# A form preference for TensorE in a list scheduler, and a shorter layer-norm step, in a hybrid decoder kernel

## The chip, the core and the metric

The kernel runs on one core of one Trainium2 chip. The metric is the device time of one execution in microseconds (us), a median over runs. Engines are named as in the profile: PE (TensorE, matrix products), PEld (its weight loads), DVE (VectorE), ACT (ScalarE), POOL (GpSimd), SP (SyncE, which here only issues DMAs).

## The reference, cut to what matters

Two layers over a sequence of 1024 tokens of width 1024, batch 1, all float32. Layer 0 mixes tokens by a gated delta rule (8 heads of 128, causal convolution of 4 taps, chunked recurrence), layer 1 by a complex diagonal state space (S5, 64 groups of 16 channels). Beside either mixer runs a cross-attention of 4 heads into 256 memory tokens. Each layer ends like this:

```python
h = jnp.concatenate([mix, cross], axis=-1) @ w_o[i]
x = layer_norm(DN_ALPHA * x + h, ln1_g[i], ln1_b[i])
f = jnp.square(jax.nn.relu(x @ mlp_w1[i])) @ mlp_w2[i]
x = layer_norm(DN_ALPHA * x + f, ln2_g[i], ln2_b[i])
```

with

```python
mu = jnp.mean(xf, axis=-1, keepdims=True)
var = jnp.mean(jnp.square(xf - mu), axis=-1, keepdims=True)
return (xf - mu) * lax.rsqrt(var + 1e-5) * g + b
```

## The kernel before, in words

**Products.** Large products are split: each float32 operand becomes a high part in float32r (a copy on ACT) and a low part (a subtraction on DVE), and `mm3` (lines 394 to 399) issues three f32r products, high by high, high by low, low by high, into one PSUM bank. PE's large products therefore stand at lines 397, 398 and 399, mostly 128x128 by 128x512. Small products of the recurrences and all transposes stay in float32 ("f32" below): the delta rule's keys, queries and values (lines 1138 to 1343), its block inverse (line 1284), its recurrence (`gdn_recur`, lines 1429, 1432, 1435, 1441, 1447), the S5 products (lines 1875, 1945, 1970, 1971) and the transposes (lines 530, 1471, 1569 and others). An f32 product appears as two rows in the trace, a transpose as one. The profile prints both f32 and f32r as f32; the line tells them apart.

**Stages.** From 0 to about 670 us runs layer 0's mixer: projections of head h+1 are woven between the steps of head h's recurrence (`weave`). A step of the recurrence is a product whose result passes through DVE (R, line 1431, and S, line 1446) or ACT (e, line 1437) before the next. To about 780 us runs the output projection, to about 820 us the first layer norm (`block_end`), where transposes feed the first products of the MLP. The MLP of layer 0 lasts to about 1440 us, with S5 tables beside it; then follow S5, its gate and the attention of layer 1, the output projection, and from about 1910 us the MLP of layer 1. Its last part, `mlp_last`, makes 16 groups of 12 products, two for each of 8 tiles (tau 0 to 7) of 128 tokens. When the second group of a tile is done, `done` in `mlp_block` (line 2340) calls `layer_norm` and sends the tile out.

**Layer norm** (line 493). Two ways give the statistics. On DVE: two `bn_stats` (L509), `bn_aggr` (L510) for mean and variance, and a step that makes 1024 (variance + 1e-5) (L511). On ACT (where `junk` is given): sums (L502) and sums of squares (L505), with small steps on DVE (L503, L506). POOL then raises this number to -1/2 (L512). DVE makes two passes over the tile, (y - mean) g (L522) and times the power, plus b (L523). The gain g has been scaled by 32 on ACT, which makes good the 1024. For the very last tile the passes are L514 and L517 (in two halves), and the DMAs out are L518. In layer 1 tiles 5 and 6 take the ACT way.

**What sets the order.** The program is first written down, and then `settle` (line 62) reorders all instructions but the first few, on all engines at once, and fixes the order on each engine. It is a list scheduler with a cost model (`price`). PE's products get a due time, which is the sum of the costs of the products ahead of them in the written program; everything else must be done by the due times of what depends on it. At each step the scheduler picks for each engine among the instructions whose inputs are known (at most 40 us of due time ahead for PE):

```python
r = max(ready[x], s, free[e], due[x] - ahead if e != E.PE else 0.0)
...
other = 1.28 if sets[x] not in (None, table) else 0.0
k = (0, due[x] + other, r, x) if r <= free[e] + 0.1 else (1, r + other, due[x], x)
```

The smallest k wins: among those that can start within 0.1 us of the engine's being free, the one due first; if there is none, the one that can start first. `other` is the price of a change of ACT's function table. (For PE there is one charge already: 0.15 us on an f32 product that would leave a single f32r product between two f32 ones.) After a pick the successors become ready:

```python
same = e == E.PE and ins[y].engine == e
ready[y] = max(ready[y], r + (0.0 if x not in deps[y] else busy if same else length + lag + (margin if ins[y].engine == E.PE else 0.0)))
```

So a successor on the same engine other than PE is taken to be ready `length` + 0.05 us after its predecessor's start, where `length` is 0.08 us (DVE) or 0.1 us (ACT) more than the time for which the engine is busy.

Of the kernel before, what the change touches and what calls it, by code (L numbers as in the profile page):

```python
# [10 lines left out]
F32 = mybir.dt.float32  # L11
F32R = mybir.dt.float32r
AF = mybir.ActivationFunctionType
# [3 lines left out]
P = 128  # L17
# [16 lines left out]
class Trunk:  # L34
    def __init__(self, ctx, tc, a):
        self.tc = tc
        self.nc = nc = tc.nc
        self.a = a
        self.uid = 0
        self.turn = 0  # L40
        self.proj = 0
        self.soon = set()
        self.home, self.fixed = {}, set()
        self.cp = ctx.enter_context(tc.tile_pool(name="cp", bufs=1))
        self.sp = ctx.enter_context(tc.tile_pool(name="sp", bufs=1))
        self.ps = ctx.enter_context(tc.tile_pool(name="ps", bufs=1, space=bass.MemoryType.PSUM))
        self.dp = ctx.enter_context(tc.tile_pool(name="dp", bufs=1, space=bass.MemoryType.DRAM))
        self.ident = self.const("ident", [P, P])
        make_identity(nc, self.ident)
        self.const("pad", [P, 112])  # L50
        self.eps_ln = self.const("eps_ln", [P, 1])
        nc.gpsimd.memset(self.eps_ln, 1024 * 1e-5)
        self.mhalf = self.const("mhalf", [P, 4])
        nc.gpsimd.memset(self.mhalf, -0.5)
        self.half = self.const("half", [P, 4])
        nc.gpsimd.memset(self.half, 0.5)
# [5 lines left out]
    def settle(self, first, last, reach=0.0, ahead=15.0, passes=1, margin=0.0, late=0.0, hold=1e3):  # L62
# [118 lines left out]
        for _ in range(passes):  # L181
# [36 lines left out]
            while len(order) < n:  # L218
                first_ = None
                drift = free[E.PE] - due[turns[head]] if head < len(turns) else 0.0  # L220
                for e in names:
                    pick = None
                    for x in open_[e]:
                        if e == E.PE and x != turns[head] and due[x] > due[turns[head]] + reach - 1e-6:
                            continue
                        s = room(x) if fresh[x] else 0.0
                        if s is None:
                            continue
                        if e == E.SP:
                            s += 1  # L230
                        r = max(ready[x], s, free[e], due[x] - ahead if e != E.PE else 0.0)
                        if cost[x][2] > 1.5:
                            r = max(r, due[x] + drift - hold)
                        if e == E.PE and kind == "fr" and ins[x].ins[0].dtype == F32:
                            r += 0.15
                        other = 1.28 if sets[x] not in (None, table) else 0.0
                        k = (0, due[x] + other, r, x) if r <= free[e] + 0.1 else (1, r + other, due[x], x)
                        if pick is None or k < pick[0]:
                            pick = k, r, x
                    if pick and (first_ is None or pick[1:] < first_[1:]):  # L240
                        first_ = pick
                assert first_, f"no order: {len(order)} of {n}"
                r, x = first_[1:]
                e = ins[x].engine
                busy, length, moves = cost[x]
                if sets[x] not in (None, table):
                    table, busy, length = sets[x], busy + 1.28, length + 1.28
                if moves:
                    served = max(served, r + length - moves) + moves
                    length = served - r + late  # L250
                if port[x]:
                    r = max(r, locked)
                    locked = r + busy
                if e == E.PE:
                    lost += r - free[e]
                    kind = (kind + "fr"[ins[x].ins[0].dtype == F32R])[-2:]
                    gone.add(x)
                    while head < len(turns) and turns[head] in gone:
                        head += 1
                open_[e].remove(x)  # L260
                free[e] = r + busy
                order.append(x)
                for nm in fresh[x]:
                    t = self.home[nm][:2]
                    slots[t].remove(min(slots[t]))
                    turn[t].remove(nm)
                for y in after[x] + then[x]:
                    same = e == E.PE and ins[y].engine == e
                    ready[y] = max(ready[y], r + (0.0 if x not in deps[y] else busy if same else length + lag + (margin if ins[y].engine == E.PE else 0.0)))
                    wait[y] -= 1  # L270
                    if not wait[y]:
                        open_[ins[y].engine].append(y)
                for nm in uses(ins[x]):
                    if nm in users:
                        over[nm] = max(over[nm], r + length + (3 if ins[x].opcode == 'DMACopy' and e == E.Pool and self.home[nm][1] == 'gb' else 0.0))
                        todo[nm] -= 1
                        if not todo[nm] and nm not in behind and self.home[nm][:2] in slots:
                            slots[self.home[nm][:2]].append(over[nm] + lag)
# [214 lines left out]
    def layer_norm(self, y, gb, junk=None, last=None):  # L493

        nc = self.nc
        st = self.tile("st", [P, 2, 6], F32, "bn")
        halves = y if isinstance(y, list) else [y[:, c * HALF:(c + 1) * HALF] for c in range(2)]
        mv = self.tile("st", [P, 4], F32, "mv")
        if junk is not None:
            s = st.rearrange("p a b -> p (a b)")  # L500
            for c in range(2):
                nc.scalar.activation(junk, halves[c], AF.Copy, accum_out=s[:, c:c + 1])  # L502
            nc.vector.tensor_scalar(mv[:, 0:1], s[:, 0:1], s[:, 1:2], -1.0 / 1024, op0=ALU.add, op1=ALU.mult)  # L503
            for c in range(2):
                nc.scalar.activation(junk, halves[c], AF.Square, bias=mv[:, 0:1], accum_out=s[:, 4 + c:5 + c])  # L505
            nc.vector.scalar_tensor_tensor(mv[:, 2:3], s[:, 4:5], s[:, 5:6], self.eps_ln, op0=ALU.add, op1=ALU.add)  # L506
        else:
            for c in range(2):
                nc.vector.bn_stats(st[:, c, :], halves[c])  # L509
            nc.vector.bn_aggr(mv[:, 0:2], st)  # L510
            nc.vector.tensor_scalar(mv[:, 2:3], mv[:, 1:2], 1024.0, 1024 * 1e-5, op0=ALU.mult, op1=ALU.add)  # L511
        nc.gpsimd.tensor_tensor(mv[:, 3:4], mv[:, 2:3], self.mhalf[:, 0:1], op=ALU.pow)  # L512
        if last is not None:
            nc.vector.scalar_tensor_tensor(y, y, mv[:, 0:1], gb[0], op0=ALU.subtract, op1=ALU.mult)  # L514
            for c in range(2):
                c = slice(c * HALF, (c + 1) * HALF)
                nc.vector.scalar_tensor_tensor(y[:, c], y[:, c], mv[:, 3:4], gb[1][:, c], op0=ALU.mult, op1=ALU.add)  # L517
                nc.sync.dma_start(last[:, c], y[:, c])  # L518
            return
        parts = [(y, slice(0, 1024))] if not isinstance(y, list) else [(y[c], slice(c * HALF, (c + 1) * HALF)) for c in range(2)]  # L520
        for o, c in parts:
            nc.vector.scalar_tensor_tensor(o, o, mv[:, 0:1], gb[0][:, c], op0=ALU.subtract if junk is None else ALU.add, op1=ALU.mult)  # L522
            nc.vector.scalar_tensor_tensor(o, o, mv[:, 3:4], gb[1][:, c], op0=ALU.mult, op1=ALU.add)  # L523
# [1816 lines left out]
    def mlp_block(self, i, B, ahead, xd, side, out, more):  # L2340
        new = []

        def done(y, tau):
            if tau == 0:
                self.gb2 = self.load_gb(self.a["ln2_g"][i:i + 1], self.a["ln2_b"][i:i + 1])
                self.nc.scalar.activation(self.gb2[0], self.gb2[0], AF.Copy, scale=32.0)
                if more:
                    new.extend(self.new_xT())
            self.layer_norm(y[tau], self.gb2, self.psum("mm", "jk") if tau in ((), (5, 6))[i] else None, last=out[tau] if tau == 7 and not more else None)
            if tau < 7 or more:  # L2350
                self.nc.sync.dma_start(out[tau], y[tau])
            if more and tau == 7:
                self.last_x(y, new, more(new))
            elif more and tau < 6:
                self.transpose_x(y[tau], tau, new)
# [91 lines left out]
```

## Time and profile before

| | |
|---|---|
| median of 3 runs | 2513.36 us (2511.43 to 2513.53) |
| the profiled execution | 2512.02 us |
| its span, first to last instruction | 2510.3 us |
| mean granted TensorE clock | 0.998 |
| instructions | 36952 |

The profile is of one execution. Its page gives, for each engine, the time for which it was busy, and follows the chain of work that ended last back from the last instruction. Matrix products overlap in PE's pipeline: a product of 512 columns shows as 0.39 us, but the next one starts about 0.23 us later, so the distance from start to start is what counts. A wait is the idle time of an engine just before an instruction, put down to the instruction that released it last. A window row gives, for a stretch of time, each engine's busy time with the number of its instructions, and the granted clock.

### The profile page before, as it was taken

To read this page: it belongs to the slowest core of one execution; us is meant where nothing else is said; L and a number is where in the kernel's file an instruction comes from. 1 tells how busy PE (TensorE), PEld (TensorE's weight loads), DVE (VectorE), ACT (ScalarE), POOL (GpSimd) and SP (SyncE) were. 2 spreads that over 40 slices of the span, in tenths; PEclk is the share of its full clock that TensorE was granted. 3 is DMA by queue.
4 is the path that set the end of the run, shared out by engine and by line. 5 is a ranking of instruction groups with operands and counts; after the bars stand their busy time and mean duration, and the time that the engine had idled before them with its cause. 6 is when DMAs were issued, how large, how long until landed. Compare 5 with 4: busy or idle time off the path is not lost.

```text
span 2510.3 us, 36952 instructions
## 1 busy us (share of the span) xinstructions
PE 2471.1 (98%) x12181; PEld 2063.9 (82%) x12181; DVE 1969.6 (78%) x3676; ACT 1283.0 (51%) x2730; POOL 435.9 (17%) x673
## 2 busy tenths in 40 slices
PE   8999999999999999999999999999999999999998
PEld 6888887887887887888888888888887888888886
DVE  7786888777779798879988957786687666578788
ACT  6665555554556576554444244564365555544441
POOL 1232332414002023212210123112011000000000
PEclk9999999999999999999999999999999999999999
DMA  6464585767854567487454489669736434574532
GB/s 211 119 163 125 138 257 135 237 189 226 270 166 157 192 218 236 154 297 240 148 161 134 157 245 301 214 216 331 259 131 206 155 143 164 216 255 133 168 105 97
DMA packets 320769, 481.17 MB, mean 192 GB/s; under 512 B 110225, under 2 KB 141153, under 8 KB 320577
## 3 DMA queue, kind: packets, MB, share of 16 engines
q1 hardware_dynamic: 293056, 423.76, 51.9%
q0 software_dynamic: 25216, 50.86, 6.9%
q10 hardware_dynamic: 2304, 4.20, 0.4%
q8 instruction: 96, 1.57, 0.3%
q14 instruction: 97, 0.79, 0.1%
HBM read 321.91 MB, written 156.73 MB: 191 GB/s over the span
## 4 chain that ended last, share of the span: by engine, by line
PE 87%; DVE 5%; ACT 3%; DMA 2%; issue 2%; POOL 1%; SPq 0%; DVEq 0%; POOLq 0%; ACTq 0%
PE q L398 7%; PE q L397 7%; PE q L399 7%; PE tm L397 4%; PE tm L399 4%; PE tm L398 4%; PE pA L399 3%; PE pA L397 3%; PE pA L398 3%; PE wi L397 3%; PE wi L399 3%; PE wi L398 3%; PE pC L399 2%; PE pC L397 2%; PE pC L398 2%; PE pB L397 2%
## 5 line engine op out<-in xcount | busy, mean ns | idle before, releaser
L397 PE MATMUL q<-wkh,hkh 128*128 128x512 f32 x784 | 306.2, 391 | 0.7 <-ACT G L1886 0.7
L398 PE MATMUL q<-wkl,hkh 128*128 128x512 f32 x784 | 305.9, 390 | 0.5 <-DVE wkl L901 0.5
L399 PE MATMUL q<-wkh,hkl 128*128 128x512 f32 x784 | 305.4, 390 | 0.0
L900 ACT CAST wkh<-wr 128x512 fp32r<-128x512 f32 x168 | 104.9, 624 | 237.5 <-PE q L398 186.2
L512 POOL TENSOR_TENSOR mv<-mv,mhalf 128x1 f32<-128x1 f32 x32 | 26.7, 833 | 858.9 <-DVE mv L511 634.6
L397 PEld LDWEIGHTS q<-wkh,hkh 128*128 128x128 f32 x784 | 147.2, 188 | 32.2 <-ACT G L1886 1.6
L398 PEld LDWEIGHTS q<-wkl,hkh 128*128 128x128 f32 x784 | 147.3, 188 | 31.0 <-DVE wkl L901 1.1
L399 PEld LDWEIGHTS q<-wkh,hkl 128*128 128x128 f32 x784 | 147.2, 188 | 30.5
L901 DVE TENSOR_TENSOR wkl<-wr,wkh 128x512 fp32r<-128x512 f32 x168 | 115.5, 688 | 65.8 <-issue 55.6
L397 PE MATMUL wi<-xTh,wih 128*128 128x512 f32 x384 | 159.9, 416 | 0.2 <-ACT qT L1098 0.2
L398 PE MATMUL wi<-xTl,wih 128*128 128x512 f32 x384 | 152.6, 397 | 0.0
L399 PE MATMUL wi<-xTh,wil 128*128 128x512 f32 x384 | 152.4, 397 | 0.0
L901 DVE TENSOR_TENSOR hkl<-hr,hkh 128x512 fp32r<-128x512 f32 x196 | 133.9, 683 | 0.2 <-ACT hkh L900 0.2
L900 ACT CAST hkh<-hr 128x512 fp32r<-128x512 f32 x196 | 120.8, 616 | 1.3 <-DMA hr<-hd 1.2
L397 PE MATMUL tm<-so 128*128 128x512 f32 x280 | 109.8, 397 | 0.0
L1621 ACT CAST so<-or 128x1024 fp32r<-128x1024 f32 x70 | 72.0, 1049 | 59.5 <-DMA or<-wod 42.0
L1622 DVE TENSOR_TENSOR so<-or,so 128x1024 fp32r<-128x1024 f32 x70 | 84.5, 1220 | 16.1 <-ACT so L1621 16.0
L398 PE MATMUL tm<-so 128*128 128x512 f32 x224 | 88.2, 394 | 0.0
L399 PE MATMUL tm<-so 128*128 128x512 f32 x224 | 87.4, 391 | 0.0
L399 PEld LDWEIGHTS wi<-xTh,wil 128*128 128x128 f32 x384 | 72.7, 189 | 14.8
L397 PEld LDWEIGHTS wi<-xTh,wih 128*128 128x128 f32 x384 | 73.2, 191 | 12.5 <-ACT qT L1098 0.6
L398 PEld LDWEIGHTS wi<-xTl,wih 128*128 128x128 f32 x384 | 73.2, 191 | 11.6 <-issue 0.3
(588 smaller groups left out, 7381.8 us busy)
## 6 DMA issues: line engine op xcount, KB each, us to landing
hr<-hd SPq DMA_DIRECT2D x212, 256.0 KB, 2.8
wr<-in_w_dram SPq DMA_DIRECT2D x56, 512.0 KB, 5.0
hd<-u SPq DMA_DIRECT2D x92, 256.0 KB, 2.0
w1r<-in_w_dram SPq DMA_DIRECT2D x32, 512.0 KB, 3.5
hd<-hid SPq DMA_DIRECT2D x60, 256.0 KB, 2.3
hd<-p SPq DMA_DIRECT2D x60, 256.0 KB, 2.2
w1r<-in_w_dram SPq DMA_DIRECT2D x56, 256.0 KB, 3.6
wir<-in_w_in_dram SPq DMA_DIRECT2D x24, 512.0 KB, 3.9
```

The source lines that it names most:

```text
L397: mm(ps, a[0], b[0], start=start, stop=False, skip_group_check=onto)
L398: mm(ps, a[0], b[1], start=False, stop=False, skip_group_check=onto)
L399: mm(ps, a[1], b[0], start=False, stop=stop, skip_group_check=onto)
L512: nc.gpsimd.tensor_tensor(mv[:, 3:4], mv[:, 2:3], self.mhalf[:, 0:1], op=ALU.pow)
L900: nc.scalar.copy(hi, s)
L901: nc.vector.tensor_tensor(lo, s, f32(hi), op=ALU.subtract)
L1621: nc.scalar.copy(hi, r)
L1622: V.tensor_tensor(lo, r, f32(hi), op=ALU.subtract)
```

## The change

It has four parts.

1. In the scheduler, a product on PE whose form (f32 or f32r, by its first operand) differs from that of the product picked last is taken to be ready 0.035 us later, and `other` is 2.0 for it. Among the products that can start now it therefore goes behind one of the same form that is due up to 2.0 us later; where nothing can start now, behind one of the same form that can start up to 2.0 us (and the 0.035) later.
2. In the scheduler, a successor on the same engine (any engine, DMA issues excepted) counts as ready 0.06 us after its predecessor's busy time, if the predecessor stands in the last 60 us of the program.
3. In `layer_norm`, a [P, 2] constant (0, 1e-5) is added to (mean, variance) in one step, which writes the mean again and the variance plus 1e-5 side by side. The factor 1024 is gone in `mlp_block`, and with it the scaling of `gb2` by 32 on ACT. In `block_end` (y given as a list of halves) the sum of squares stays unscaled. Both passes read the mean from where the new step writes it; on the DVE way the first pass therefore comes behind this step.
4. In `mlp_block` of layer 1 tiles 3, 4 and 5 take the ACT way, instead of 5 and 6.

```diff
+        self.eps2 = self.const("eps2", [P, 2])
+        nc.gpsimd.memset(self.eps2[:, 0:1], 0.0)
+        nc.gpsimd.memset(self.eps2[:, 1:2], 1e-5)
...
                         other = 1.28 if sets[x] not in (None, table) else 0.0
+                        if e == E.PE and kind[-1:] != "fr"[ins[x].ins[0].dtype == F32R]:
+                            r, other = r + 0.035, 2.0
                         k = (0, due[x] + other, r, x) if r <= free[e] + 0.1 else (1, r + other, due[x], x)
...
-                    same = e == E.PE and ins[y].engine == e
-                    ready[y] = max(ready[y], r + (0.0 if x not in deps[y] else busy if same else length + lag + (margin if ins[y].engine == E.PE else 0.0)))
+                    same = ins[y].engine == e and (e == E.PE or not moves and spot[x] > now - 60.0)
+                    ready[y] = max(ready[y], r + (0.0 if x not in deps[y] else busy + (0.0 if e == E.PE else 0.06) if same else length + lag + (margin if ins[y].engine == E.PE else 0.0)))
...
-        mv = self.tile("st", [P, 4], F32, "mv")
+        mv = self.tile("st", [P, 6], F32, "mv")
...
-            nc.vector.scalar_tensor_tensor(mv[:, 2:3], s[:, 4:5], s[:, 5:6], self.eps_ln, op0=ALU.add, op1=ALU.add)
+            if isinstance(y, list):
+                nc.vector.scalar_tensor_tensor(mv[:, 1:2], s[:, 4:5], s[:, 5:6], self.eps_ln, op0=ALU.add, op1=ALU.add)
+            else:
+                nc.vector.tensor_scalar(mv[:, 4:5], s[:, 4:5], s[:, 5:6], 1.0 / 1024, op0=ALU.add, op1=ALU.mult)
+                nc.vector.tensor_tensor(mv[:, 1:2], mv[:, 4:5], self.eps2[:, 1:2], op=ALU.add)
...
-            nc.vector.bn_aggr(mv[:, 0:2], st)
-            nc.vector.tensor_scalar(mv[:, 2:3], mv[:, 1:2], 1024.0, 1024 * 1e-5, op0=ALU.mult, op1=ALU.add)
-        nc.gpsimd.tensor_tensor(mv[:, 3:4], mv[:, 2:3], self.mhalf[:, 0:1], op=ALU.pow)
+            nc.vector.bn_aggr(mv[:, 4:6], st)
+            nc.vector.tensor_tensor(mv[:, 0:2], mv[:, 4:6], self.eps2, op=ALU.add)
+        nc.gpsimd.tensor_tensor(mv[:, 3:4], mv[:, 1:2], self.mhalf[:, 0:1], op=ALU.pow)
...
-                self.nc.scalar.activation(self.gb2[0], self.gb2[0], AF.Copy, scale=32.0)
...
-            self.layer_norm(y[tau], self.gb2, self.psum("mm", "jk") if tau in ((), (5, 6))[i] else None, last=out[tau] if tau == 7 and not more else None)
+            self.layer_norm(y[tau], self.gb2, self.psum("mm", "jk") if tau in ((), (3, 4, 5))[i] else None, last=out[tau] if tau == 7 and not more else None)
```

## The prediction

> **What bounds the kernel.** I read the page first: how long, which engine, which chain.
>
> ```profile
> span 2510.3 us, 36952 instructions
> PE 2471.1 (98%) x12181; PEld 2063.9 (82%) x12181; DVE 1969.6 (78%) x3676; ACT 1283.0 (51%) x2730; POOL 435.9 (17%) x673
> PE 87%; DVE 5%; ACT 3%; DMA 2%; issue 2%; POOL 1%; SPq 0%; DVEq 0%; POOLq 0%; ACTq 0%
> ```
>
> PE is busy 98% of the span and holds 87% of the chain that ended last. A change of order removes no product, so it can win only what lies between the products. Second, the stages: a window without any f32 product, and the two windows in which the granted clock fell.
>
> ```profile
> 1910.00:2456.00 546.00, 545.77 (x2407) 451.35 (x2405) 382.74 (x609) 268.28 (x470) 0.00 (x0) 1.00 0.50 171
> 440.00:443.50 3.50, 3.50 (x15) 3.02 (x14) 2.82 (x7) 2.36 (x10) 3.50 (x7) 0.53 0.70 167
> 576.70:580.10 3.40, 2.79 (x11) 2.62 (x12) 3.31 (x6) 1.90 (x4) 3.02 (x5) 0.50 0.97 251
> ```
>
> Columns are the stretch, its length, then each engine's busy time with its count (PE first), and behind them the granted clock. An f32r product of 512 columns takes 546.00/2407 = 0.2268 us back to back, and that stage (MLP of layer 1) leaves nothing to win. The other two rows are half clock: 3.4 us each, so 1.7 us lost each.
>
> Third, the waits of PE, longest first; columns are total, times, longest.
>
> ```profile
> PE ba L1011 <- ACT xTh L993: 7.9, 2, 7.2
> PE po L1432 <- ACT on L1460: 4.3, 5, 2.4
> PE pe L1435 <- DVE R L1431: 3.0, 1, 3.0
> ...
> PE pe L1435 <- ACT e L1437: 0.6, 1, 0.6
> ```
>
> 7.2 us are the load of the input before the first product; the change does not touch that. The rest is mostly the recurrence of the gated delta rule (lines 1429 to 1447), f32 products in a chain through DVE and ACT, woven with f32r projections.
>
> **The change, part by part.** All durations are from the profiled execution: 2512.02 us, of which 2510.3 is the span. The median of the three runs, 2513.36, lies 1.34 above it; I take the sum off the median.
>
> *1. Fewer changes of form.* What does a change cost? One return (f32r, six f32 rows, f32r), and a long stretch of f32 alone:
>
> ```profile
> 432.02 0.61 PE L1319 MATMUL qt<-ident,qT 128*128 128x128 f32 x4
> 432.48 0.39 PE L1429 MATMUL ks<-S,kT 128*128 128x128 f32 x2
> 432.62 0.48 PE L399 MATMUL wi<-xTh,wil 128*128 128x512 f32 x1
> 432.93 0.40 PE L397 MATMUL wi<-xTh,wih 128*128 128x512 f32 x1
> ...
> 1479.07 0.38 PE L1970 MATMUL py<-s5t 128*128 128x128 f32 x2
> ...
> 1482.42 0.39 PE L1971 MATMUL py<-r,H 128*128 128x127 f32 x2
> ```
>
> From 1479.07 to 1482.42 stand 30 f32 rows, so 0.1117 us each. Six of them and one f32r product should take 6 x 0.1117 + 0.2268 = 0.897 us. From 432.02 to the second f32r product at 432.93 it took 0.91. The shown gap moves (the last f32 row seems to take 0.03, the next f32r product 0.31), but the whole return costs only about 0.013 us. The scheduler books 0.035 for each change, 0.07 for a return.
>
> PE's timeline has 342 such returns. The first and last groups of f32 are:
>
> ```profile
> 41.34 0.41 PE L1058 MATMUL gc<-early 128*128 128x64 f32 x2
> ...
> 1903.06 0.66 PE L530 MATMUL xt<-ident,y 128*128 128x128 f32 x4 [0.59 <-DVE xB L535]
> ```
>
> All of them together are worth 342 x 0.013 = 4.4 us, the end of what this part can give by itself. The rule lets a product wait while one of the other form is due within 2.0 us, so two f32 groups can merge if at most 2.0/0.2268 = 8 f32r products stand between them. 169 groups in the timeline are so placed: 2.2 us at most. Many are steps of one recurrence, where the second needs the first through ACT or DVE, and these cannot merge: 0 at least. I take half: **-1.1 us**.
>
> *2. Short waits on the recurrence.* With more slack a product can come into its place in time. The rows of two waits, one with f32r work at hand and one without:
>
> ```profile
> 264.21 0.46 PE L1435 MATMUL pe<-mix,iv 128*128 128x128 f32 x2 [0.57 <-ACT e L1437]
> ...
> 264.65 0.48 PE L399 MATMUL wi<-xTh,wil 128*128 128x512 f32 x1
> ...
> 502.44 0.49 PE L1432 MATMUL po<-S,gb 128*128 128x128 f32 x2 [0.88 <-ACT on L1460]
> ```
>
> At 264.21 the written order put a step of the chain ahead of projections that ran 0.44 us later: PE stood 0.57 us though there was work. Under the rule, in the midst of f32r products, the step goes behind them and its wait is covered. Of the waits above this holds for 0.6 (pe), and for po for 4.3 - 2.4 - 0.88 = 1.0: together 1.6 us. It is 0 if the f32r products are due more than 2.0 us later. I take two thirds: **-1.1 us**. What goes late instead is the chain itself; that is the second rival.
>
> *3. The end of the kernel: layer norm.* The last rows of DVE and of POOL; the first two columns are start and duration:
>
> ```profile
> 2499.94 1.28 DVE L522 SCALAR_TENSOR_TENSOR y<-y,mv,gb 128x1024 f32<-128x1024 f32 x1
> 2501.14 0.69 DVE L938 TENSOR_TENSOR y<-tm,y 128x512 f32<-128x512 f32 x1
> 2501.74 1.28 DVE L523 SCALAR_TENSOR_TENSOR y<-y,mv,gb 128x1024 f32<-128x1024 f32 x1
> 2502.93 0.69 DVE L509 BATCH_NORM_STATS2 bn<-y 128x6 f32<-128x512 f32 x1
> 2503.65 0.21 DVE L510 BATCH_NORM_AGGREGATE mv<-bn 128x2 f32<-128x12 f32 x1
> 2503.90 1.28 DVE L514 SCALAR_TENSOR_TENSOR y<-y,mv,gb 128x1024 f32<-128x1024 f32 x1
> 2505.10 0.15 DVE L511 TENSOR_SCALAR mv<-mv 128x1 f32<-128x1 f32 x1
> 2505.97 1.41 DVE L517 SCALAR_TENSOR_TENSOR y<-y,mv,gb 128x512 f32<-128x512 f32 x2 [0.73 <-POOL mv L512]
> ```
>
> ```profile
> 2500.17 1.46 POOL L512 TENSOR_TENSOR mv<-mv,mhalf 128x1 f32<-128x1 f32 x1 [5.08 <-DVE mv L506]
> 2505.39 0.55 POOL L512 TENSOR_TENSOR mv<-mv,mhalf 128x1 f32<-128x1 f32 x1 [3.76 <-DVE mv L511]
> ```
>
> The last add (2501.14) waits for no one but DVE; behind it stands the second pass of the tile before (2501.74, 1.19 us to the next start), then the statistics, the first pass L514, the eps step L511, the power on POOL, and L517, which starts 4.83 us after the add. The change does two things here. The bookkeeping for dependent steps on one engine in the last 60 us becomes 0.06 us, so the statistics count as ready right after the add and the second pass of the other tile no longer slips in between. And the eps step now comes ahead of L514, since it also writes the mean that L514 reads.
>
> New chain: add, statistics after 0.72 (as from 2502.93 to 2503.65), aggregate after 0.72, eps after 0.25 (as from 2503.65 to 2503.90), L514 after 0.25, together 1.94. The power beside a pass is slow: at 2500.17 it ended at 2501.63, 0.41 us after the pass that began at 2499.94 (end 2501.22). So L517 comes 1.28 + 0.41 = 1.69, with 0.03 to start 1.72, after L514, where it came 2.07 before. Sum 3.66 against 4.83: -1.2 if the displaced second pass finds a place ahead of the add, and with 1.20 us for it inside the chain 4.86, no gain. With the old order and only the eps step moved, 0.25 more and 0.35 less: -0.1. So 0 to -1.2; DVE is nearly full there, so I take the middle, **-0.6 us**.
>
> [...]
>
> The choice of tiles whose sums go to ACT (3, 4, 5 instead of 5, 6) takes one pair of statistics off DVE and gives tile 6 back to it; PE has no wait in the last 44 us, so only the tail sees it, inside the same 0 to -1.2.
>
> *4. The scaling of the layer-norm gain is gone.*
>
> ```profile
> L2346 ACT ACTIVATE gb<-gb x2: 1057/1058/1058, 1304.4 to 2429.8; 128x1024 f32<-128x1024 f32 x2
> ```
>
> Twice 1.06 us of ACT, 49% idle, and nobody waits for it (no wait on it in the views): 0. If that cover were gone, 2.1 us. The two further memsets of POOL lie ahead of the first load, under the 7.2 us: 0. The 0.035 in the scheduler is bookkeeping and issues nothing.
>
> **Sum**: -1.1 - 1.1 - 0.6 = -2.8, so 2513.4 - 2.8 = **2510.6**. Bounds of the terms: -(2.2 + 1.6 + 1.2) = -5.0 to 0. A new order also moves other waits under 1 us, on which I put +-2.5 as an estimate from the waits listed above: 2506 to 2515.
>
> **The rivals.**
>
> *The long stalls go too.* The waits of 2.4 and 3.0 us stand in the recurrence; if the new order happens to feed PE there, they and both half-clock windows go: 2.4 + 3.0 + 2 x 1.7 = 8.8, with the sum 2501.8. Against it: in the 3.0 us the wait is for DVE, and nothing in the rule speeds DVE.
>
> *Slower: the chain is held back.* The rule makes a step of the recurrence wait up to 2.0 us behind f32r products that are due later, even when it is the step on which everything else in that head hangs. When PE has nothing ready at all, the key adds the same 2.0 us, so it may idle for a product of its own form while one of the other form is ready sooner. While projections last, the delay is covered; where they run out, it becomes a stall. That happens now in six places (five waits of po, one of pe). Four held 2.0 us are 8.0; where a wait of about 0.9 grows past 2.4, the half clock follows, at two places 3.4. With parts 1 and 3: 8.0 + 3.4 - 1.7 = +9.7, 2523.1. It decides against the change from about three full holds and one loss of clock (7.7 us). For it: chain products wait longest now. Against it: a step overdue by more than 2.0 us still goes first.
>
> *Nothing moves.* Dependent f32 groups cannot merge and the order stays: only the tail, -0.1: 2513.3.
>
> *Longer runs of transposes cost clock.* A run of f32 transposes might count as rest, and each block end lose 1.7 us: +3.4 - 2.8, 2514.0. [...] The trace does not bear it out, within its lengths: at the end of the first block PE runs almost nothing but transposes for over 3 us (a timeline row, then the window, 20 PE rows), at a granted clock of 1.00.
>
> ```profile
> 802.88 1.25 PE L530 MATMUL xt<-ident,y 128*128 128x128 f32 x8 [0.26 <-DVE xB L535]
> ```
>
> ```profile
> 801.00:804.20 3.20, 2.68 (x20) 2.02 (x19) 2.76 (x5) 3.20 (x8) 2.57 (x3) 1.00 0.88 293
> ```
>
> **Chances.** About 0.2% (5 us) is what a measurement of this kernel can tell from no change: 2508.3 to 2518.4. The forecast 0.44 (0.30 within, 0.14 below, its range reaching there); long stalls gone 0.15, faster; chain held back 0.29, slower; nothing moves 0.10 and transposes 0.02, both within. Faster 0.29, same 0.42, slower 0.29. The range 2501 to 2523 leaves out less than half of the second case and of the third, 0.18 together. The forecast's own range is 2506 to 2515.
>
> **What would show it.** Part 1: PE's timeline has some 255 returns instead of 342. Part 2: the wait of pe on e and the short ones of po are gone. Part 3: the eps step stands ahead of the last L514, L517 starts about 4.2 us after the last add. Wrong: a wait of PE in the recurrence above 2 us that was below 1, a third window at half clock, or waits at the block ends (780 to 820, 1880 to 1910) grown by over 2 us.

## The result, and the profile after

| | before | after |
|---|---|---|
| median | 2513.45 us (2511.04 to 2516.41, 6 runs) | 2531.73 us (2527.41 to 2534.05, 6 runs) |
| ratio, 95% interval | | 1.0073 [1.0061, 1.0084] |
| span of the profiled execution | 2510.3 us | 2531.2 us |
| returns on PE (f32r, f32 rows, f32r) | 342 | 295 |

The change makes the kernel slower by 0.73%. The forecast was 2510.6, so its sign is wrong, and 2531.7 lies above the range, which ended at 2523. Lines of the changed kernel are the old ones plus 3 to 9.

The head of the page after:

```profile
span 2531.2 us, 36989 instructions
PE 2481.3 (98%) x12181; PEld 2066.2 (82%) x12181; DVE 1971.7 (78%) x3677; ACT 1288.9 (51%) x2736; POOL 435.0 (17%) x675
PE 82%; DVE 8%; DMA 5%; ACT 2%; issue 2%; SPq 1%; POOL 0%; POOLq 0%; DVEq 0%; ACTq 0%
```

PE issues the same 12181 rows. What grew on the chain that ended last is DVE (5% to 8%) and DMA (2% to 5%). The waits of PE after (total, times, longest; po, ks and pe are results of the recurrence's products, p and py of those of S5, xt of the transposes at the ends of the blocks):

```profile
PE po L1441 <- ACT on L1469: 4.5, 3, 2.2
PE p L1954 <- DMA s5t<-ud: 4.4, 3, 1.9
PE xt L539 <- DVE xB L544: 3.4, 5, 0.9
PE py L1980 <- DVE wql L369: 2.1, 1, 2.1
...
PE ks L1438 <- DVE S L1455: 1.5, 1, 1.5
...
PE pe L1444 <- ACT e L1446: 0.4, 1, 0.4
```

Three places speak. The recurrence (po, ks, pe) is not quieter, as the forecast had it. The transposes of the block ends (xt) wait five times, where it was three times and 1.4 us. And S5 (p, py), which the prediction's forecast and rivals don't name, waits for transfers (p, 4.4 us) and once for a step on DVE (py, 2.1 us).

To put sizes on it I walked PE's timeline. Each product has a time that it takes back to back (0.227 us for 512 columns, as in the prediction's window; 0.111 us for an f32 row). What the distance to the next start has beyond this is PE's loss at that place: a wait, a slow clock, a change of form. Summed by stage, in us, for five kernels (the three in the middle have parts of the change alone, below):

| stage (time before) | before | ln_only | pref_only | shift_only | after |
|---|---|---|---|---|---|
| front (7 to 202) | 5.9 | 4.7 | 7.4 | 5.6 | 6.5 |
| recurrence (202 to 637) | 24.1 | 23.5 | 34.8 | 22.9 | 30.2 |
| S5 (1463 to 1646) | 1.8 | 8.5 | 2.2 | 17.2 | 11.9 |
| gate and attention (1646 to 1750) | 0.1 | 0.1 | 1.1 | 0.3 | 1.3 |
| block end 1 (1750 to 1909) | 5.2 | 5.1 | 7.4 | 5.9 | 7.8 |
| last product to end of span | 9.95 | 9.42 | 9.95 | 9.41 | 9.42 |

Of the 20.9 us by which the span grew, S5 has 10.1, the recurrence 6.1, block end 1 2.6, gate and attention 1.2; the rest are parts below 0.7, and the end gains 0.5. Slow clock is a part of these sums: between 50 us and the last product, 17.0 us of the profiled execution after ran at half clock (13.6 in the recurrence, 3.4 in S5). In the one before it was 6.8 us (granted clock 0.50 from 440.2 to 443.6; products of 512 columns start 0.42 to 0.43 us apart there, in place of 0.227), so 5.1 us of the 20.9 are clock.

S5 in windows; first the kernel before, then after (the last three columns are granted clock, DMA share, GB/s):

```profile
1520.00:1560.00 40.00, 40.00 (x237) 35.30 (x236) 27.64 (x52) 19.14 (x30) 13.30 (x19) 1.00 1.04 318
1560.00:1600.00 40.00, 40.00 (x229) 35.00 (x229) 27.68 (x52) 19.62 (x32) 11.68 (x17) 1.00 0.99 292
```

```profile
1520.00:1560.00 40.00, 36.44 (x208) 31.62 (x207) 25.69 (x48) 16.80 (x26) 11.27 (x17) 1.00 0.90 281
1560.00:1600.00 40.00, 36.78 (x203) 32.29 (x202) 24.22 (x44) 18.33 (x29) 12.64 (x19) 0.96 1.02 303
```

Before, PE was full here, but so were the DMA engines (1.04 and 0.99): PE waited for nothing, and the transfers had no reserve.

The end of the span, on DVE:

```profile
2520.86 2.46 DVE L532 SCALAR_TENSOR_TENSOR y<-y,mv,gb 128x1024 f32<-128x1024 f32 x2
2523.24 0.69 DVE L947 TENSOR_TENSOR y<-tm,y 128x512 f32<-128x512 f32 x1
2523.96 0.69 DVE L518 BATCH_NORM_STATS2 bn<-y 128x6 f32<-128x512 f32 x1
2524.69 0.21 DVE L519 BATCH_NORM_AGGREGATE mv<-bn 128x2 f32<-128x12 f32 x1
2524.93 0.16 DVE L520 TENSOR_TENSOR mv<-mv,eps 128x2 f32<-128x2 f32 x1
2525.13 1.28 DVE L523 SCALAR_TENSOR_TENSOR y<-y,mv,gb 128x1024 f32<-128x1024 f32 x1
2526.85 1.41 DVE L526 SCALAR_TENSOR_TENSOR y<-y,mv,gb 128x512 f32<-128x512 f32 x2 [0.44 <-POOL mv L521]
```

The second passes of the other tiles (2520.86) stand ahead of the last add, the eps step stands ahead of the first pass, and the last pass starts 3.61 us after the add, where it was 4.83.

### The profile page after: what moved, and what is told of

It reads as the page before. It is cut to its first block, busy times and chain, and to the rows that moved or that the text cites. A ratio compares the mean times of both kernels' runs of the same rounds, so it can differ in the third digit from the quotient of the medians.

```text
span 2531.2 us, 36989 instructions
## 1 busy us (share of the span) xinstructions
PE 2481.3 (98%) x12181; PEld 2066.2 (82%) x12181; DVE 1971.7 (78%) x3677; ACT 1288.9 (51%) x2736; POOL 435.0 (17%) x675
## 4 chain that ended last, share of the span: by engine, by line
PE 82%; DVE 8%; DMA 5%; ACT 2%; issue 2%; SPq 1%; POOL 0%; POOLq 0%; DVEq 0%; ACTq 0%
PE q L403 7%; PE q L402 7%; PE q L404 7%; PE tm L402 4%; PE tm L403 4%; PE tm L404 4%; PE pA L404 3%; PE pA L402 3%; PE pA L403 3%; PE wi L402 3%; PE wi L404 3%; PE wi L403 3%; PE pC L404 2%; PE pC L402 2%; PE pC L403 2%
## 5 line engine op out<-in xcount | busy, mean ns | idle before, releaser
L1631 DVE TENSOR_TENSOR so<-or,so 128x1024 fp32r<-128x1024 f32 x70 | 84.0, 1220 | 10.1 <-ACT so L1630 9.9
```

The source lines that it names most:

```text
L1631: V.tensor_tensor(lo, r, f32(hi), op=ALU.subtract)
```

## The experiments

All ratios are to the kernel before on the same chip. Two kernels whose instructions stand in the same order on every engine are called the same order.

### The two halves

`ln_only` is the changed kernel without the preference:

```diff
-                        if e == E.PE and kind[-1:] != "fr"[ins[x].ins[0].dtype == F32R]:
-                            r, other = r + 0.035, 2.0
```

> The layer-norm parts and the 60 us rule alone, without the form preference. If the preference is the whole loss (first theory), this is at or a little under the kernel before: 2510 to 2514 us, the S5 stage and the recurrence as before, and only the tail some 0.5 us shorter. If the layer-norm parts carry a part of the loss (rival), it is above 2516 us.

Measured: 2517.65 us, 1.0024 [1.0014, 1.0033]. `pref_only` is the kernel before with these two lines and nothing else.

> The form preference alone on the kernel before. First theory (the preference is the whole loss): 2527 to 2535 us, with the waits of the S5 products on the load of u (4.4 us in the changed kernel) and three more windows at half clock. Rival (the loss needs both, or comes from a reshuffle that any change of the costs sets off): the time is far from that, under 2522 us, and other stages carry it.

Measured: 2523.71 us, 1.0046 [1.0031, 1.0061]. `pref_no_shift` is the changed kernel with `other = 2.0` and without the 0.035.

> The changed kernel with the preference in the key (2.0), but without the 0.035 us by which a change of form is booked later. If holding products back is what costs, this is as slow as the changed kernel, 2527 to 2535 us. If it is the booked time that moves side work (loads, sums on DVE) against PE in the S5 stage, the S5 waits on the load of u go and it is 9 to 11 us faster, about 2521 us.

Measured: 2524.26 us, 1.0049 [1.0034, 1.0064]. `shift_only` has `r = r + 0.035` alone.

> The changed kernel with the 0.035 us booked, but no preference in the key. If holding products back costs, this is at the kernel before, 2510 to 2515 us. If the booked time moves side work in the S5 stage, the S5 loss of 9 to 11 us stands: about 2521 us.

Measured: 2523.45 us, 1.0043 [1.0028, 1.0058].

`shift_only` came out where the booked time alone was to cost, at about 2521. `pref_only` and `pref_no_shift` fell between the times that their two theories had, and decide for neither.

So both halves lose, at different places. The recurrence loses only with the 2.0 in it (26.0 us in `pref_no_shift`, whose column isn't in the table), and most with the 0.035 as well. S5 loses in all kernels that have the layer-norm part (7.5 us in `pref_no_shift`; of the 17.2 in `shift_only`, 5.1 are three stretches of 3.4 us at half clock). `ln_only` is among them, and there the order in S5 is that of the kernel before. Its waits there:

```profile
PE p L1952 <- DMA s5t<-ud: 2.5, 2, 1.7
PE py L1978 <- DMA H<-h1d: 2.2, 3, 1.5
```

The kernel before has no such wait. The same work in the same order, and transfers come late: that is neither the preference nor the layer norm's arithmetic. What is left is where things lie. The new constant `eps2` has 8 bytes for each partition and gets a slot of 32 in the built program, so every tile allocated behind it moves up by 32 bytes. Before, the large tiles started at multiples of 512 (an unused tile `pad` of 112 columns sees to it); after, at 32 past one.

### Addresses

Four kernels move the tiles of the kernel before and do nothing else (same order). This is all of the first:

```diff
-        self.const("pad", [P, 112])
+        self.const("pad", [P, 120])
```

> The kernel before with nothing changed but the unused tile `pad`, 120 columns in place of 112. Each engine gets the same instructions in the same order; only the SBUF addresses of all later tiles are 32 bytes higher, as they are in the changed kernel, where the new constant `eps2` takes a slot of 32 bytes. Theory A (the changed kernel's loss in the stage of `p`, L1949 and after, is one of addresses: every large tile then starts 32 bytes past a multiple of 512, packets take longer, and the stage whose transfers only just arrive in time loses): 2516 to 2520 us, packets of 4096 bytes at 204 to 207 ns in place of 199.4, TensorE's idle time in that stage 5 to 17 us in place of 1.8. Rival B (the loss there comes from the layer norm's new instructions or from the order of the work): 2511 to 2515 us as before, packets as before.

> The kernel before with `pad` of 128 columns: later tiles 64 bytes higher, the same instructions in the same order. If transfers mind whether a row starts on a multiple of 64 bytes only: 2511 to 2515 us, packets as before (199.4 ns for 4096 bytes). If they mind a multiple of 128, 256 or 512: 2516 to 2520 us and slower packets, as with 32 bytes. Rival B (addresses don't matter): 2511 to 2515 us, and no loss in the kernel shifted by 32 bytes either.

> The kernel before with `pad` of 144 columns: later tiles 128 bytes higher, the same instructions in the same order. So far: 32 bytes 2520.0 us, 64 bytes 2517.2, 256 bytes 2513.5 (no loss). If a multiple of 128 is enough: 2511 to 2515 us, 1 to 3 us of idle TensorE in the stage of p. If it takes 256: 2515 to 2518 us, 3 to 6 us idle there.

> The kernel before with `pad` of 176 columns: later tiles 256 bytes higher, large tiles at 256 past a multiple of 512, the same instructions in the same order. 32 bytes higher gave 2520.0 us, 64 bytes 2517.2. If a multiple of 256 is enough for the transfers: 2511 to 2515 us, and TensorE's idle time in the stage of p at 1 to 3 us. If it takes 512: 2516 to 2519 us, 4 to 7 us idle there.

Each ratio is to the kernel before on the same chip; the 0 row is from the chip of the moves by 32 and 64 bytes.

| tiles moved by | us | ratio | S5 beyond back to back | packets of 4096 bytes, mean ns | packet time, all, over 16 engines |
|---|---|---|---|---|---|
| 0 (before) | 2513.06 | 1 | 1.8 | 199.4 | 1496.0 |
| 32 bytes | 2520.02 | 1.0027 [1.0016, 1.0038] | 7.4 | 204.1 | 1508.1 |
| 64 bytes | 2517.21 | 1.0018 [1.0010, 1.0027] | 5.8 | 202.0 | 1504.1 |
| 128 bytes | 2516.72 | 1.0016 [1.0007, 1.0026] | 6.9 | 202.0 | 1509.0 |
| 256 bytes | 2513.50 | 0.9997 [0.9988, 1.0006] | 1.8 | 197.1 | 1486.7 |

Moves by 32, 64 and 128 bytes cost 3.7 to 7 us; the move by 256 costs nothing. The transfers of S5 in the window from 1440 to 1660 (queue, count, size, median us from issue to landing); the kernel before, moved by 32 bytes, moved by 256:

```profile
tab<-tabd POOLq DMA_DIRECT2D x23, 256.0 KB, 6.8
ud<-s5t SPq DMA_DIRECT2D x8, 512.0 KB, 3.5
s5t<-ud SPq DMA_DIRECT2D x8, 512.0 KB, 10.3
```

```profile
tab<-tabd POOLq DMA_DIRECT2D x23, 256.0 KB, 8.3
ud<-s5t SPq DMA_DIRECT2D x8, 512.0 KB, 5.0
s5t<-ud SPq DMA_DIRECT2D x8, 512.0 KB, 11.7
```

```profile
tab<-tabd POOLq DMA_DIRECT2D x23, 256.0 KB, 6.2
ud<-s5t SPq DMA_DIRECT2D x8, 512.0 KB, 3.7
s5t<-ud SPq DMA_DIRECT2D x8, 512.0 KB, 10.3
```

With 32 bytes they take 1.4 to 1.5 us longer each; with 256 they are within 0.6 us of the kernel before, none of them slower by more than 0.2. PE's waits with 32 bytes are those of `ln_only`, for the tables H and for s5t:

```profile
PE py L1971 <- DMA H<-h1d: 2.6, 2, 1.5
PE p L1945 <- DMA s5t<-ud: 1.1, 1, 1.1
```

On average the packets of 4096 bytes take 2.4% longer at 32 bytes than in the kernel before, 1.3% longer at 64 and 128, and 1.2% less at 256. Their medians are 159 ns in all five, so the loss is among the slower ones: a tenth of them took over 301 ns in the kernel before and over 322 ns in the changed kernel, whose median is 159 too. Why is open. The means move a little from kernel to kernel: 197.1 to 200.0 ns in all whose tiles stand at the old addresses or 256 bytes on, 204.1 to 206.1 in all that are 32 bytes off. So 32 bytes cost most, and the 1.3% is known only roughly.

The counter-test puts the changed kernel's tiles back (`pad` of 104 columns, the same order as without that): without the preference (`ln_pad104`) and whole (`after_pad104`).

> The changed kernel without the two lines of the preference (the layer norm's part, `eps2` and the short DVE estimate alone), and `pad` of 104 columns, so that all tiles behind the constants stand at the addresses that they have in the kernel before. Theory A (addresses): the loss of 5 us that this part alone showed goes, and the gain at the end (0.5 us) is left: 2510 to 2513 us, packets at 199 to 200 ns, 1 to 3 us of idle TensorE in the stage of `p`. Rival B (the new instructions or their order cost it): 2516 to 2519 us as without the move.

> The changed kernel, whole, with `pad` of 104 columns: same instructions in the same order, the large tiles at the addresses of the kernel before. Theory A (two losses that add: the preference's, some 10 us, and the addresses', 5 to 10 us): 2521 to 2525 us, the level of the preference alone (2523.7) less the 0.5 us at the end, and 1 to 3 us of idle TensorE in the stage of `p` in place of 11.9. Rival B (addresses don't matter): 2529 to 2533 us as the changed kernel.

Measured: `ln_pad104` 2511.92 us, 0.9995 [0.9986, 1.0004], S5 at 2.6 us; `after_pad104` 2519.47 us, 1.0027 [1.0016, 1.0037], S5 at 2.2 us. Both as the theory of addresses had it, the second a little below its interval. Taken off in this order, addresses are 1.0073 - 1.0027 = 0.46% of the 0.73%, or 11.6 us, and the preference is 1.0027 - 0.9995 = 0.32%, or 8 us; the layer-norm part itself gains about what was forecast for it, too little to tell from nothing. Each difference has two intervals in it and is good to about 0.15%, or 4 us. And the split depends on the order: by `pref_only` the preference alone is 0.46%, and 1.0073 - 1.0046 = 0.27%, or 7 us, is left for what comes on top, which is what 32 bytes cost alone. So either cause is worth some 7 to 12 us, and which one is larger isn't shown.

### The preference, at the old addresses

The next kernels are all `after_pad104` with one edit. First the rival of the prediction, that the steps of the recurrence are held back (`chain_free`; the condition is added to the line that sets `other`):

```diff
+ and ins[x].outs[0].bass_ap.tensor.name[:3] not in ("po_", "ks_", "pe_", "pS_")
```

> The changed kernel with the tiles at their old addresses (`pad` of 104 columns: 2519.5 us), and the preference doesn't apply to the f32 products of the recurrence's chain (the tiles ks, pe, pS and po): they are taken as before, and the fill work alone is sorted by form. Theory C (the loss of 7.5 us that the preference has at old addresses comes from holding these steps back, each by up to 2 us): 2511 to 2514 us, TensorE's time beyond back-to-back in the recurrence back to 24 us from 28.6. Rival D (the loss comes from the fill work: sorted by form it is spent at other places, loads and vector steps stand in another order in their queues, and the chain waits for those): 2517 to 2521 us, 27 to 30 us in the recurrence, and long waits for po, pe or ks at other places than before.

Measured: 2520.58 us, 1.0029 [1.0019, 1.0040]; the recurrence is at 29.7 us. A smaller worth (`r, other = r + 0.035, 0.5`):

> The changed kernel with the tiles at their old addresses, and a preference worth 0.5 us of due time in place of 2.0. Theory C (steps held back by up to the preference's worth): the loss shrinks with it, to 2512 to 2515 us. Rival D (any other order of the fill work loses about as much, whatever the worth): 2516 to 2522 us, not in proportion.

Measured: 2515.00 us, 1.0009 [1.0000, 1.0018]. One direction only, holding f32r products after an f32 one (`kind[-1:] == "f"` and the product f32r):

> The changed kernel with the tiles at their old addresses, and the preference in one direction alone: after an f32 product the f32r products are held back, after an f32r product nothing is. No step of the recurrence is held then; f32 work is drawn together behind each step. Theory C (held steps of the chain): no loss, 2510 to 2514 us. Rival D (fill work moved): 2515 to 2521 us, since f32r fill work, the only long work that covers the chain's waits, is what moves.

Measured: 2515.07 us, 1.0009 [1.0000, 1.0018]. The other one, holding f32 products after an f32r one:

> The changed kernel with the tiles at their old addresses, and the preference in the other direction alone: after an f32r product the f32 products (all steps of the recurrence among them) are held back by up to 2.0 us, after an f32 product nothing is. Theory C (held steps of the chain): the whole loss is here, 2518 to 2523 us. Rival D: a loss that may be larger or smaller than the other direction's, 2513 to 2521 us, with its long waits behind a load or a vector step that stands ahead in its queue.

Measured: 2511.13 us, 0.9991 [0.9982, 1.0000]; 310 returns, the recurrence at 24.0 us.

Theory C falls. The chain is free in `chain_free` and the loss is all there; in `stay_f32r` every step of the chain can be held by 2.0 us and there is no loss. What C has for itself is the dose: 0.5 costs less than 2.0, and 2515.00 lies where C had it, below D's 2516 to 2522. But at 0.5 the order has 339 returns, so hardly any groups have merged at all. Staying among f32r products (310 returns) costs nothing that can be told; staying among f32 products (320) costs 0.14% against `ln_pad104`, just clear of the intervals; the two together (295) cost 0.32%. In the recurrence neither direction alone loses: from its first to its last product it is 24.9 us in `ln_pad104`, 23.4 in `stay_f32`, 23.9 in `stay_f32r`, and 28.6 with both. So rival D, which fits `chain_free` and `stay_f32`, isn't shown to be the mechanism there.

By stage (`x0` is the first product of the output projection): `pref_rec` applies the preference to `x < x0`, `pref_rest` to `x >= x0`.

> The changed kernel with the tiles at their old addresses, and the preference for those products alone that the program issues before the first output projection (the recurrence, with its projections). Theory D by stage (of the preference's 7.5 us, 4.6 sit in the recurrence, the rest at the end of the second block and around it): 2515 to 2518 us, the second block's end at 5.5 us beyond back-to-back in place of 7.4. Rival G (the stages aren't separate, what follows depends on how the order before it came out): the second block's end or other stages lose too, 2518 to 2522 us.

> The changed kernel with the tiles at their old addresses, and the preference for those products alone that the program issues from the first output projection on. Theory D by stage: the recurrence at 24 us beyond back-to-back, as without a preference, the end of the second block at 7.4 us in place of 5.5: 2513 to 2516 us. Rival G: 2510 to 2513 us, or a loss in the recurrence, whose fill work is in part of later stages.

Measured: 2518.43 us, 1.0019 [1.0010, 1.0027], and 2515.01 us, 1.0006 [0.9997, 1.0014]. The two losses over `ln_pad104` (0.24% and 0.11%) make up the whole one (0.32%) within their intervals. That fits separate stages, though 2518.43 is 0.4 us above what was expected for them. At the end of block 1 PE waits, in `pref_rest`, `pref_rec`, `stay_f32` and `stay_f32r`:

```profile
PE xt L540 <- DVE xB L545: 2.3, 3, 0.9
```

```profile
PE xt L540 <- DVE xB L545: 0.6, 1, 0.6
```

```profile
PE xt L539 <- DVE xB L544: 2.3, 3, 0.9
```

```profile
PE xt L539 <- DVE xB L544: 0.7, 1, 0.7
```

The kernel before has 0.6 there, once. So this loss comes with staying in f32 (over the ends of both blocks the same wait is 4.8 us in `stay_f32`, 4.6 in `pref_rest`, 1.4 before), and the timeline of `after_pad104` shows how:

```profile
1894.87 0.63 PE L539 MATMUL xt<-ident,y 128*128 128x128 f32 x4
1896.19 0.30 PE L539 MATMUL xt<-ident,tw 128*128 128x128 f32 x1 [0.69 <-DVE xB L544]
1899.08 0.49 PE L539 MATMUL xt<-ident,tw 128*128 128x128 f32 x3
```

Four transposes, then one of the next four, for which PE waits 0.69 us until DVE has read the bank; then twelve f32r products, and only then the other three. In the kernel before, these groups stand whole, in fours, with f32r products between:

```profile
1893.46 0.60 PE L530 MATMUL xt<-ident,tw 128*128 128x128 f32 x4
```

As I read these rows, the preference makes PE stand for a product of the form just used while the other form has work, as the prediction's slower rival said of the second half of the key.

In the recurrence the new long wait is one for po at 371 us. PE and DVE in `after_pad104`:

```profile
370.81 0.49 PE L1441 MATMUL po<-S,gb 128*128 128x128 f32 x2 [2.51 <-ACT on L1469]
```

```profile
367.11 0.62 DVE L1128 SCALAR_TENSOR_TENSOR D<-gb,scr 128x128 f32<-128x128 f32 x2 [2.37 <-DMA gb<-gcd]
367.64 0.16 DVE L1465 SCALAR_TENSOR_TENSOR scr<-scr 128x4 f32<-128x4 f32 x1
```

PE waits for ACT's copy `on`, that for POOL's power, that for DVE's L1465, and this stands behind a decay step (L1128) whose load is 2.4 us late: its 5 us from issue to landing began only at 362.1, behind other issues on SP. `d_later` puts the decay steps behind L1465, at this one place; `chain_first` puts the whole chain (L1465, the power, `on`, the residual R) ahead of what needs the load, on each engine. (Their lines are higher by 8 to 10 and by 21 to 24.)

> The changed kernel with the tiles at their old addresses, and in the finished order two vector steps change places with one: the first two of the four decay steps (L1128) that stand on DVE just ahead of a recurrence scale step (L1465) are put just behind it. It is one place in the program, at 365 us, where DVE waits 2.4 us for the load gb<-gcd with the scale step queued behind it, and TensorE then waits 2.5 us for po. Theory E (this third long wait is the order's doing: a step that waits for its load stands ahead of one that the chain needs): the wait of 2.5 us at 371 us goes or falls below 0.8 us, and the time falls by 2 to 4 us, to 2515.5 to 2517.5 us. Rival F (the wait moves to the next step in line): 2518.5 to 2520.5 us.

> The changed kernel with the tiles at their old addresses, and at the one place at 365 us the chain's steps put first on every engine: the scale step (L1465), its power on POOL and the four copies `on` (L1469) ahead of the decay steps and of their exponential, which all need the late load gb<-gcd, and the product of decay and gain (L1161) behind the next residual (L1440). Moving the DVE steps alone cut the wait for po from 2.5 to 1.6 us, because the exponential stood ahead of `on` on ACT, and the time stayed. Theory E: with ACT's order mended too, the waits for po and pe at 371 us fall below 0.5 us together, and the time to 2516 to 2518 us. Rival F (the chain is as late at the next place, where PE waits for po 2.4 us at 444 us anyway): 2518.5 to 2520.5 us, with the later waits grown by as much as this one shrank.

Measured: `d_later` 2519.65 us, 1.0027 [1.0018, 1.0036]. The wait is 1.6 us now, for ACT had the exponential of the same decay ahead of `on`:

```profile
366.51 0.63 ACT L1138 ACTIVATE D<-D 128x512 f32<-128x512 f32 x1 [2.34 <-DVE D L1136]
367.25 0.63 ACT L1119 ACTIVATE th<-qT 128x512 f32<-128x512 f32 x1
367.79 1.12 ACT L1479 ACTIVATE on<-po,scr 128x128 f32<-128x128 f32 x4
```

`chain_first`: 2518.22 us, 1.0022 [1.0012, 1.0031]. Here the wait for po at that place is gone, and 0.5 us for R are left:

```profile
369.25 0.41 PE L1464 MATMUL po<-S,gb 128*128 128x128 f32 x2
370.19 0.46 PE L1467 MATMUL pe<-R,iv 128*128 128x128 f32 x2 [0.53 <-DVE R L1463]
```

Of 2.5 us of wait, 2.0 are taken away, and the median falls by 1.3, which these intervals can't tell from nothing. `d_later` came out at rival F's time, `chain_first` between E's and F's. The wait is explained (two queues, one late load), but it isn't the recurrence's loss: `stay_f32r` waits at the same place and loses nothing there.

```profile
371.51 0.49 PE L1441 MATMUL po<-S,gb 128*128 128x128 f32 x2 [2.21 <-ACT on L1469]
```

F's mechanism, later waits that grow by as much, isn't seen either. All waits of PE over 0.05 us from 195 to 640 us are 10.4 us in the kernel before, 13.0 in `after_pad104`, 10.5 in `d_later` and 11.1 in `chain_first`. What grew is slow clock: 6.8 us of the recurrence ran at half clock in the kernel before and in `after_pad104`, 13.6 in `d_later`, 10.2 in `chain_first`. That took back 3.4 and 1.7 us in the profiled executions. One place, in `after_pad104` and in `d_later`, which differ in two rows of DVE and in nothing else (third from last is the granted clock):

```profile
437.70:447.90 10.20, 5.85 (x26) 4.78 (x27) 7.88 (x19) 6.91 (x26) 10.17 (x16) 0.87 0.56 149
437.70:447.90 10.20, 8.50 (x27) 6.83 (x28) 7.13 (x16) 5.68 (x20) 10.19 (x19) 0.50 0.52 142
```

## Why the prediction was wrong

*What bounds the kernel.* PE does, before and after. The reading stopped one step early: it went by PE's waits, S5 had none before, and its DMA share of 1.04 and 0.99 was not looked at as a limit.

*Part 1, fewer changes of form: -1.1.* The count went the way forecast, by about half: 295 returns instead of 255, so 47 x 0.013 = -0.6. That they gain even this no run shows. The 0.013 is read off one return; over 258 returns without a wait in the trace before, the same sum has a median of 0.001 and a mean of 0.005 us (0.003 and 0.014 with the step into the group). All of these are small beside what the new order costs.

*Part 2, short waits: -1.1. This step failed in sign.* It counted the waits that a new order covers and put those that it opens at nothing, but for the second rival. The wait of pe on e went from 0.6 only to 0.4, the waits of po from 4.3 to 4.5, and at old addresses all waits of PE from 195 to 640 us from 10.4 to 13.0. The preference doesn't know which product has work behind it to cover a wait; that it moved f32r work away from where it covered something is argued here, not shown. At old addresses, the preference costs 8 us: recurrence 28.6 us in place of 24.0, block end 1 7.4 in place of 5.5, gate and attention 1.2 in place of 0.1 (`after_pad104` against `ln_pad104`).

*Part 3, the end: -0.6.* Right, -0.5 (9.95 to 9.42 us from the last product to the end). The chain behind the add is the one drawn, 3.61 us where 3.66 was worked out as the best; the other tiles' second passes did find their place ahead of it, and in return the add comes 1.44 us after the last product instead of 0.78.

*Part 4, and the constant. This is the other step that failed.* "The two further memsets of POOL lie ahead of the first load, under the 7.2 us: 0" priced the constant as an instruction. It is also an allocation, and it moved every later tile by 32 bytes, which alone cost 7 us in the kernel before (1.0027). Price: 7 to 12 us. Nothing in the prediction had a place for it, which is why the time lies above the range: with the old addresses it was 2519.5, inside. The scaling of the gain at nothing was right as far as `ln_pad104` can tell.

*The rivals.* The slower one (2523.1) has nearly the preference's own time (2523.7 in `pref_only`), but that is luck: its main mechanism, held steps of the chain, is refuted by `chain_free` and `stay_f32r`. Its second, PE standing for its own form, is what the block end shows. More windows at half clock came, as its sign foresaw; those at 371 and at 1590 us have no counterpart before:

```profile
370.90:374.30 3.40, 2.73 (x14) 2.69 (x15) 2.87 (x6) 3.37 (x14) 0.73 (x2) 0.71 0.47 179
447.20:450.60 3.40, 3.40 (x15) 3.21 (x15) 1.18 (x6) 2.57 (x11) 3.40 (x8) 0.50 0.66 180
584.00:587.40 3.40, 3.14 (x12) 2.88 (x13) 3.02 (x7) 1.81 (x4) 1.77 (x4) 0.51 0.89 180
1590.30:1593.70 3.40, 3.40 (x20) 3.40 (x20) 0.00 (x0) 0.60 (x1) 0.00 (x0) 0.58 1.03 348
```

*What stays open:* why the recurrence loses only with both directions together, how far the slow clock of a single profiled execution stands for all of them, and why packets get slower by the amounts that they do. A preference in the due time alone, without the second half of the key, wasn't tried.

No version beats the kernel before clearly. `stay_f32r` beats the changed kernel by 0.8% and stands against the one before at 0.9991, at the edge of its interval.

## What to carry to other kernels

Look at a stage without waits for its second limit: here the DMA share was at 1.0, and packets slower by 2.4% on average turned 1.8 us of loss into 7.4. A new constant is an allocation as well as an instruction; work out what it does to the addresses of all that is allocated behind it, and run the old kernel with nothing but the shift when a time moves and the order doesn't. In a list scheduler, a bonus for the cheap neighbour is paid by what that order would have covered: here 47 returns, worth 0.6 us by the forecast, were bought with 8 us or more, while the direction that lost nothing (`stay_f32r`) saved 32 of the 47.

## What the hardware showed that wasn't expected

The addresses are the first: no engine's instruction changed, and 32 bytes cost 7 us.

The clock is the second. `pref_only` and `after_pad104` have the same order on PE over the whole recurrence and the same wait of 2.5 us for po at 371 to 372 us. Behind it the granted clock was, in `pref_only`:

```profile
372.40:379.40 7.00, 7.00 (x29) 6.42 (x30) 4.37 (x8) 3.79 (x16) 2.78 (x5) 0.54 0.67 216
```

and in `after_pad104`:

```profile
370.80:377.80 7.00, 6.99 (x42) 6.27 (x43) 6.40 (x12) 4.36 (x17) 2.78 (x5) 1.00 0.67 210
```

42 rows against 29 in the same 7 us: one wait cost 2.5 us, the other 2.5 and some 3.2 of slow clock. The prediction's rule (a wait past 2.4 us brings half clock) is too simple; whether a wait does is not in its length alone. In the changed kernel the wait at this place was shorter, 1.80 us, and half clock came behind it (granted clock 0.51 from 372.4 to 375.8 us):

```profile
371.57 0.49 PE L1441 MATMUL po<-S,gb 128*128 128x128 f32 x2 [1.80 <-ACT on L1469]
```

In all traces here, every stretch at half clock between 50 us and the last product is 3.4, 6.8 or 10.2 us long: two of 3.4 in the kernel before, three of 3.4 and one of 6.8 in the changed one, the one of 10.2 above in `d_later`. No run shows what sets these lengths, or why the same wait was followed by half clock in one kernel and not in the other. In the recurrence the profiled execution of `pref_only` has 20.4 us at half clock and that of `after_pad104` 6.8, which is 6.8 us of time. So a part of the difference between the medians of these two kernels (2523.71 and 2519.47, intervals that overlap) may be slow clock and not the order.
